# The output projection of a hybrid encoder block: every block product with both halves of the activations in one matrix multiplication, and part of VectorE's work on GpSimd

## Chip, cores, metric

One core of one Trainium2 chip. The metric is the device time of one execution in microseconds (us); the time of the kernel before is the median of 3 runs. Engines are named as in the profile: PE is TensorE, PEld its weight loads, DVE is VectorE, ACT is ScalarE, POOL is GpSimd, SP issues DMAs.

## The reference

One layer of a streaming encoder on x of 512 frames by 2048 columns, all in float32. The part that the change touches is the second of these lines, the projection by W_out with its residual, and what the next line needs of it:

```python
mixed = jnp.concatenate([o_gdn, o_rwkv], axis=-1).astype(h.dtype)
h = h + mixed @ w_out[l]
h = h + _cross_attention(_rmsnorm(h, norm_xattn[l]), _rmsnorm(mem, norm_mem[l]), ...)
```

`_rmsnorm` divides by the root of the mean of h squared over the 2048 columns, so the sum of squares of the new h has to be there when cross-attention's scores are done.

## The kernel before

All large matrix products use float32 numbers split in a high part (rounded to the type that PE multiplies fast) and a low part, the rest. A product is then high x high, high x low and low x high. ACT makes the high part (`S.copy`, line 130), DVE the low part by a subtraction (line 131).

**The output projection** is one stage. It makes h transposed, in 8 blocks `p` of 256 output columns by 512 frames. Each block is a Strassen product of 2 x 2 parts (`strassen`, from line 1334): 7 products with the constants B11, T1, T2, T3, T4, B22, B21 take the place of 8. The weight operands of the products are the four loaded parts a11, a21, a22, a12, 128 x 1024 each, and four sums of them: s1 = a21 + a22, s2 = s1 - a11, a11 - a21 (written over a21) and s4 = a12 - s2. The activation operands `comb[i][k]` (`ob` in the trace) are made ahead, 128 x 512 each: columns 0 to 255 hold the high part of 256 frames, columns 256 to 511 the low part.

**A product** (`product`) splits its weight operand into `whi` and `wlo` (three buffers each), then PE goes over 8 pieces k of 128 rows. The PSUM tile `op` is 128 x 512. There are two forms. A *narrow* product multiplies `whi` by the high half and by the low half of `ob` in two instructions of 256 columns that add into the same 256 columns of `op`. A *wide* one (its number is in `wide`) multiplies `whi` by all 512 columns in one instruction, so that the two partial results lie in the two halves of `op`, and whoever reads the product has to add both. Last, both forms multiply `wlo` by the high half, 256 columns. Before, B11, T2 and T3 of blocks 1 to 6 are wide, all others narrow.

**The results** are two tiles c1 and c2 per block (tiles `h` in the trace), made by DVE from the products, 256 columns at a time (`plus`, `add`, line 1380), one addition for each half that a product has; T1's result is added twice. ACT copies the first half of B11's result (line 1398). When the first half of a tile is complete as the last one, `gained` adds x (the residual, tile `sl`, line 1582), ACT squares the sum into a tile `sl` (line 1588) and DVE adds that to `acc` (line 1589). In the last block (`p == 7`) ACT and DVE also begin to split h for the scores (`second`, lines 133 and 134).

**What sets the order.** In this stage no order is written out by hand: a scheduler places the instructions on each engine when the kernel is built, and each engine then takes its own strictly in that order. Waits come from data and from buffers that turn: 3 for `whi` and `wlo`, 3 for a11 and a21 (`wraw`), 3 for a22 and a12 (`wraw2`), 2 for the sums s1, s2 and s4 (`ws`), 3 for `sl`, 2 PSUM banks for each tag. So s4 of a block lies where s1 lay, and s1 of the next block where s2 lay. POOL has no work in this stage.

Of the kernel before, what the change touches and what calls it, by code (L numbers as in the profile page):

```python
# [11 lines left out]
AF = mybir.ActivationFunctionType  # L12
ALU = mybir.AluOpType
# [60 lines left out]
def build(tc, I, out):  # L74
    nc = tc.nc
    V, S, GP, PE = nc.vector, nc.scalar, nc.gpsimd, nc.tensor
# [41 lines left out]
    def psb(nm, tag="mx", bufs=2):  # L118
        return tile_of(ps, [P, 512], F32, tag, nm, bufs)

    def mm(o, l, r, start=True, stop=True, again=False):
        PE.matmul(o, l, r, start=start, stop=stop, skip_group_check=again)  # L122
# [5 lines left out]
    def split(src, hi, lo, gain=None):  # L128
        if gain is None:
            S.copy(hi, src)  # L130
            V.tensor_tensor(out=lo, in0=src, in1=hi.bitcast(F32), op=ALU.subtract)  # L131
        else:
            S.activation(hi, src, AF.Copy, scale=gain)
            V.scalar_tensor_tensor(out=lo, in0=src, scalar=gain, in1=hi.bitcast(F32),
                                   op0=ALU.mult, op1=ALU.subtract)
# [227 lines left out]
    def tl(tag, w=512, bufs=1, shape=None):  # L363
        cnt[0] += 1
        return tile_of(pm, shape or [P, w], F32, tag, f"{tag}_{cnt[0]}", bufs)
# [50 lines left out]
    wq += [("w", I["wqT"][n][:, g * 1024:(g + 1) * 1024]) for n in range(KD) for g in range(2)]  # L416
    NKP, NKQ = 2 * NIN, 2 * NIN + 2 * KD
    raws, halves, used, whole, piece = {}, {}, set(), set(), {}

    def pieceload(i):  # L420
# [59 lines left out]
    acc = tl("r")  # L480
# [809 lines left out]
    hres = [hp[k // 4 * 2 + k % 2][:, k // 2 % 2] for k in range(16)]  # L1290
# [4 lines left out]
    def sl2(w=512):  # L1295
        cnt[0] += 1
        return ph.tile([P, 512], F32, tag="sl", name=f"sl{cnt[0]}", bufs=3)[:, 0:w]
# [10 lines left out]
    B11, T1, T2, T3, T4, B22, B21 = range(7)  # L1308
# [28 lines left out]
    def strassen(nm, pool, src, ks, done, used=None, first=False, wide=(), sums=None):  # L1337

        w = len(ks) * P

        def raw(p_, tag, bufs, i):
            cnt[0] += 1
            r = p_.tile([P, 1024], F32, tag=tag, name=f"{tag}_{cnt[0]}", bufs=bufs)[:, 0:w] \
                if p_ is pw else p_.tile([P, pool[1]], F32, tag=tag, name=f"{tag}_{cnt[0]}", bufs=bufs)[:, 0:w]
            if i is not None:
                nc.sync.dma_start(r, src[i])
            return r  # L1350

        def product(i, tag, a):
            cnt[0] += 1
            hi = pw.tile([P, 1024], F32R, tag="whi", name=f"whi{cnt[0]}", bufs=NWS)[:, 0:w]
            lo = pw.tile([P, 1024], F32R, tag="wlo", name=f"wlo{cnt[0]}", bufs=NWS)[:, 0:w]
            split(a, hi, lo)
            pt = psb(f"{nm}_{i}", tag)
            pa_ = pt[:, HA]
            last = len(ks) - 1
            for zs in (range(last), range(last, last + 1)) if first else (range(last + 1),):  # L1360
                for z in zs:
                    k, sl = ks[z], slice(z * P, z * P + P)
                    if i in wide:
                        mm(pt, hi[:, sl], comb[i][k], start=z == 0, stop=False)
                    else:
                        mm(pa_, hi[:, sl], comb[i][k][:, HA], start=z == 0, stop=False)
                        mm(pa_, hi[:, sl], comb[i][k][:, HB], start=False, stop=False)
                for z in zs:
                    mm(pa_, lo[:, z * P:z * P + P], comb[i][ks[z]][:, HA], start=False, stop=z == last)
            if used:  # L1370
                used(i)
            return (pa_, pt[:, HB]) if i in wide else (pa_,)

        def plus(o, a, p, op=ALU.add):
            for x in p:
                add(o, a, x, op)
                a = o

        def add(o, a, b, op=ALU.add):
            V.tensor_tensor(out=o, in0=a, in1=b, op=op)  # L1380

        def wraw2(i):
            return raw(pool[0], "wraw2", 3, i)

        def ws():
            return raw(pool[0], "ws", 2, None)

        a11 = raw(pw, "wraw", NWR, 0)
        if first:
            a12, a22 = raw(pw, "wraw", NWR, 3), raw(pw, "wraw", NWR, 2)  # L1390
            a21 = wraw2(1)
        else:
            a21 = raw(pw, "wraw", NWR, 1)
            a22, a12 = wraw2(2), wraw2(3)
        p1 = product(B11, "mx", a11)
        c1 = sums[0] if sums else sl2()
        c11, c12 = u1, u4 = c1[:, HA], c1[:, HB]
        S.copy(u1, p1[0])
        for x in p1[1:]:
            add(u1, u1, x)  # L1400
        if first:
            p2 = product(B21, "mg", a12)
            p4 = product(T4, "mx", a22)
        s1 = ws()
        add(s1, a21, a22)
        p5 = product(T1, "mg", s1)
        s2 = ws()
        add(s2, s1, a11, ALU.subtract)
        p6 = product(T2, "mm", s2)
        c2 = sums[1] if sums else sl2()  # L1410
        c21, c22 = u3, u2 = c2[:, HA], c2[:, HB]
        plus(u2, u1, p6)
        if first:
            plus(c11, u1, p2)
        plus(u4, u2, p5)
        add(a21, a11, a21, ALU.subtract)
        p7 = product(T3, "mm", a21)
        plus(u3, u2, p7)
        plus(c22, u3, p5)
        done(1, HB, c2)  # L1420
        if not first:
            p4 = product(T4, "mx", a22)
        plus(c21, u3, p4)
        done(1, HA, c2)
        s4 = ws()
        add(s4, a12, s2, ALU.subtract)
        p3 = product(B22, "mg", s4)
        plus(c12, u4, p3)
        done(0, HB, c1)
        if not first:  # L1430
            p2 = product(B21, "mm", a12)
            plus(c11, u1, p2)
        done(0, HA, c1)
# [13 lines left out]
    def spread(*which):  # L1447
        for i, k in which:
            comb[i][k] = (btile if k < 3 or i == B21 and k < 6 else act_tile)(f"ob{i}_{k}")
            place(i, k, *pair[k])  # L1450
# [100 lines left out]
            S.activation(sq, hres[n], AF.Square)  # L1551
            V.tensor_tensor(out=acc, in0=acc, in1=sq, op=ALU.add)

    hh_, hl_, sqsum = [], [], []

    def second(n):
        hi, lo = act_tile(f"hh{n}"), act_tile(f"hl{n}")
        split(hres[n], hi, lo, col("norm_xattn", n))
        hh_.append(hi)
        hl_.append(lo)  # L1560

    for p in range(8):
        xs = [None, None]

        def used(i):
            if i == T1:
                if p == 0:
                    spread((B22, 6), (B22, 7))
                for j in (1, 0):
                    xs[j] = sl2()  # L1570
                    nc.sync.dma_start(xs[j], I["xT"][:, 2 * p + j, :])
            elif i == T2 and p == 0:
                spread((B21, 6), (B21, 7))
                sqsum.append(ph.tile([P, T], F32, tag="acc", name="acc1", bufs=1))
            if p == 7 and i in (T2, T3):
                for n in range(2) if i == T2 else range(2, 4):
                    second(n)

        def gained(j, half, c):
            if half is HB:  # L1580
                return
            V.tensor_tensor(out=c, in0=c, in1=xs[j], op=ALU.add)
            acc = sqsum[0]
            if p == 0 and j:
                S.activation(acc, c, AF.Square)
            else:
                sq = sl2()
                S.activation(sq, c, AF.Square)
                V.tensor_tensor(out=acc, in0=acc, in1=sq, op=ALU.add)

        strassen(f"op{p}", (pz, 1024), [I["w_out"][p, i] for i in range(4)], list(range(8)), gained, used,
                 wide=(B11, T2, T3) if 0 < p < 7 else (), sums=hres[2 * p:2 * p + 2])
    pz_cm.__exit__(None, None, None)
    pl_cm = tc.tile_pool(name="pl", bufs=1, reuse_waits="tile")
    pl = pl_cm.__enter__()
# [103 lines left out]
    acc = ph.tile([P, T], F32, tag="acc", name="acc2", bufs=1)  # L1699
# [75 lines left out]
    xs = lambda u: range(2 * u[3], 2 * u[3] + 2) if len(u) > 3 else range(4)  # L1775
    units = [("u", p, 0) for p in range(32)] + [("d", e, m, *y) for e in range(4) for m in range(2) for y in (((0,), (1,)) if (e, m) in INSITU else ((),))]
    raws, sums, halves = {}, {}, {}
# [641 lines left out]
```

## Time and profile before

| what | us |
|---|---|
| median of 3 runs (2904.82, 2906.90, 2906.92) | 2906.9 |
| the profiled execution | 2904.46 |
| its span, first to last instruction | 2902.7 |
| the output projection in it, from 1305 to 1465 | 160 |

The profile is of one execution. Its page gives the busy time of each engine, and the trace behind it answers views: busy time by windows of time, groups of instructions by line, who waited for whom, the chain of work that ended last, and a timeline of single instructions. In a timeline row stand the start in us from the span's start, the duration in us (of all instructions of the row), the engine, the line, the operation, the tiles as output<-inputs with buffer numbers left out, and in brackets the idle time ahead of it with what ended it. On an engine the next instruction may start while the one before still ends, so that the price of one in a row of many is the distance from start to start.

### The profile page before, as it was taken

The page shows a single profiled execution, that of the slowest core. Times are in us where ns is not written, and L with a number is a line of the kernel's source. Part 1 is how long each engine was busy: PE and PEld are TensorE (multiplying, and loading weights), DVE is VectorE, ACT ScalarE, POOL GpSimd, SP SyncE. Part 2 cuts the span into 40 slices and gives each one's busy share as a digit, 9 for nine tenths or more (in the row PEclk, how much of TensorE's full clock was granted, in tenths as well). Part 3 has the DMA queues.
Part 4 walks back from the last instruction along what each step waited for, and adds up shares of the span by engine and source line. Part 5 has one row for each costly group of instructions (what it writes and reads, how often), then busy time and mean ns, then how long its engine had stood idle before and what let it go on. Part 6 is the DMA issues. An engine that isn't in the chain of part 4 may idle for free.

```text
span 2902.7 us, 49242 instructions
## 1 busy us (share of the span) xinstructions
PE 2870.4 (99%) x18794; PEld 2420.3 (83%) x18794; DVE 2330.4 (80%) x3547; ACT 1570.0 (54%) x2233; POOL 223.6 (8%) x547
## 2 busy tenths in 40 slices
PE   8999999999999999999999999999999999999998
PEld 7877877787877888889988888888888888888887
DVE  7787787787887877769956898898998878787888
ACT  6454555555655655564445656555555645454544
POOL 0213213213223000000000000000000000000000
PEclk9999999999999999999999999999999999999999
DMA  5646656656666788784423354565566868978733
GB/s 190 175 139 184 164 156 181 160 150 187 176 163 188 219 249 280 227 286 159 127 92 95 106 163 152 193 199 193 186 201 191 283 225 278 295 257 272 270 100 109
DMA packets 319773, 553.02 MB, mean 191 GB/s; under 512 B 100968, under 2 KB 186220, under 8 KB 319536
## 3 DMA queue, kind: packets, MB, share of 16 engines
q1 hardware_dynamic: 292144, 518.41, 58.0%
q10 hardware_dynamic: 27392, 31.46, 3.1%
q8 instruction: 147, 2.41, 0.3%
q14 instruction: 90, 0.74, 0.1%
HBM read 443.45 MB, written 106.31 MB: 189 GB/s over the span
## 4 chain that ended last, share of the span: by engine, by line
PE 93%; DMA 3%; DVE 2%; ACT 1%; issue 1%; POOL 0%; ACTq 0%; SPq 0%; DVEq 0%; POOLq 0%
PE py L256 22%; PE mxu L256 12%; PE mgu L256 6%; PE mgd L256 6%; PE mxd L256 6%; PE op L122 6%; PE vp L122 3%; PE sc L122 3%; PE at L122 3%; PE mmd L256 3%; PE kp L256 3%; PE mmu L256 3%; PE scrd L256 3%; PE scgd L256 3%; PE kq L256 3%; PE vo L122 1%
## 5 line engine op out<-in xcount | busy, mean ns | idle before, releaser
L256 ACT CAST whi<-wraw 128x1024 fp32r<-128x1024 f32 (+1 forms) x366 | 383.7, 1049 | 399.8 <-PE py L256 146.8
L256 DVE TENSOR_TENSOR wlo<-wraw,whi 128x1024 fp32r<-128x1024 f32 (+1 forms) x366 | 450.4, 1231 | 102.7 <-ACT whi L256 92.9
L256 PE MATMUL py<-xhi,whi 128*128 128x512 f32 x928 | 372.2, 401 | 7.8 <-ACT xhi L256 7.8
L256 PE MATMUL py<-xlo,whi 128*128 128x512 f32 x928 | 373.7, 403 | 0.0
L256 PE MATMUL py<-xhi,wlo 128*128 128x512 f32 x928 | 372.9, 402 | 0.0
L256 ACT CAST whi<-w 128x1024 fp32r<-128x1024 f32 x176 | 185.4, 1054 | 203.9 <-PE mxu L256 48.3
L256 DVE TENSOR_TENSOR wlo<-w,whi 128x1024 fp32r<-128x1024 f32 x176 | 214.8, 1221 | 51.5 <-ACT whi L256 49.5
L256 PE MATMUL mxu<-cb,whi 128*128 128x512 f32 x1016 | 255.0, 392 | 0.0
L256 PEld LDWEIGHTS py<-xhi,whi 128*128 128x128 f32 x928 | 175.0, 189 | 42.1 <-ACT xhi L256 7.8
L256 PEld LDWEIGHTS mxu<-cb,whi 128*128 128x128 f32 x1016 | 182.8, 189 | 32.7
L256 PEld LDWEIGHTS py<-xlo,whi 128*128 128x128 f32 x928 | 175.0, 189 | 35.5 <-DVE xlo L256 0.9
L256 PEld LDWEIGHTS py<-xhi,wlo 128*128 128x128 f32 x928 | 175.1, 189 | 35.1 <-issue 1.8
L131 DVE TENSOR_TENSOR wlo<-wraw,whi 128x1024 fp32r<-128x1024 f32 x112 | 136.6, 1221 | 45.5 <-ACT whi L130 42.5
L130 ACT CAST whi<-wraw 128x1024 fp32r<-128x1024 f32 x112 | 117.7, 1051 | 85.5 <-PE op L122 29.1
L256 PEld LDWEIGHTS mxu<-cb,wlo 128*128 128x128 f32 x1016 | 138.7, 190 | 10.5 <-DVE wlo L256 0.7
L256 PE MATMUL mxu<-cb,wlo 128*128 128x256 f32 x1016 | 142.2, 282 | 0.3 <-DVE wlo L256 0.3
L256 ACT ACT_TABLE_LOAD x87 | 111.6, 1283 | 36.4 <-DVE suml_gn L256 15.5
L256 PE MATMUL mgu<-cb,whi 128*128 128x512 f32 x512 | 129.4, 394 | 1.4 <-ACT whi L256 1.3
L256 PE MATMUL mxd<-whi,cb 128*128 128x512 f32 x512 | 126.7, 389 | 0.0
L256 PE MATMUL mgd<-whi,cb 128*128 128x512 f32 x512 | 126.5, 389 | 0.0
L256 ACT CAST whi<-ws 128x1024 fp32r<-128x1024 f32 x75 | 78.9, 1052 | 75.4 <-PE mgu L256 49.2
L122 PE MATMUL op<-ob,whi 128*128 128x256 f32 (+1 forms) x752 | 115.3, 304 | 0.0
(946 smaller groups left out, 6452.3 us busy)
## 6 DMA issues: line engine op xcount, KB each, us to landing
wraw<-in_w_in SPq DMA_DIRECT2D x116, 512.0 KB, 4.5
wraw<-in_w_up SPq DMA_DIRECT2D x65, 512.0 KB, 3.8
w<-in_w_up SPq DMA_DIRECT2D x63, 512.0 KB, 3.9
ds<-in_w_dm SPq DMA_DIRECT2D x128, 205.0 KB, 4.0
sd_s<-ds SPq DMA_DIRECT2D x128, 205.0 KB, 5.2
wraw<-sd_s SPq DMA_DIRECT2D x51, 512.0 KB, 5.1
w<-sd_s SPq DMA_DIRECT2D x50, 512.0 KB, 5.0
w<-in_w_dm SPq DMA_DIRECT2D x48, 512.0 KB, 5.1
```

The lines of the kernel that those rows point to most:

```text
L122: PE.matmul(o, l, r, start=start, stop=stop, skip_group_check=again)
L130: S.copy(hi, src)
L131: V.tensor_tensor(out=lo, in0=src, in1=hi.bitcast(F32), op=ALU.subtract)
L256: f(*a, **k)
```

## The change

Every product of every block is wide, those of blocks 0 and 7 too. POOL computes two of the four weight sums, a11 - a21 and s4, which are also written earlier in the code: a11 - a21 right behind s1, s4 right behind the product T2. For blocks 0 to 6 POOL also adds the residual and adds the squares to `acc`; block 7 keeps both on DVE. The squares are no longer issued with the residual: they are put in a list, and issued behind the next product B22 or T2. The first square of all goes to `acc` directly.

```diff
@@ strassen
         s1 = ws()
         add(s1, a21, a22)
+        GP.tensor_tensor(out=a21, in0=a11, in1=a21, op=ALU.subtract)
         p5 = product(T1, "mg", s1)
         s2 = ws()
         add(s2, s1, a11, ALU.subtract)
         p6 = product(T2, "mm", s2)
+        s4 = ws()
+        GP.tensor_tensor(out=s4, in0=a12, in1=s2, op=ALU.subtract)
...
-        add(a21, a11, a21, ALU.subtract)
         p7 = product(T3, "mm", a21)
...
-        s4 = ws()
-        add(s4, a12, s2, ALU.subtract)
         p3 = product(B22, "mg", s4)
@@ used
         def used(i):
+            if i in (B22, T2):
+                for f in later:
+                    f()
+                later.clear()
@@ gained
-            V.tensor_tensor(out=c, in0=c, in1=xs[j], op=ALU.add)
-            acc = sqsum[0]
-            if p == 0 and j:
-                S.activation(acc, c, AF.Square)
+            G = GP if p < 7 else V
+            G.tensor_tensor(out=c, in0=c, in1=xs[j], op=ALU.add)
+
+            def squared():
+                if not sqsum[1:]:
+                    sqsum.append(1)
+                    S.activation(sqsum[0], c, AF.Square)
+                else:
+                    sq = sl2()
+                    S.activation(sq, c, AF.Square)
+                    G.tensor_tensor(out=sqsum[0], in0=sqsum[0], in1=sq, op=ALU.add)
+
+            if p < 7:
+                later.append(squared)
             else:
-                sq = sl2()
-                S.activation(sq, c, AF.Square)
-                V.tensor_tensor(out=acc, in0=acc, in1=sq, op=ALU.add)
+                squared()

         strassen(...,
-                 wide=(B11, T2, T3) if 0 < p < 7 else (), sums=hres[2 * p:2 * p + 2])
+                 wide=range(7), sums=hres[2 * p:2 * p + 2])
```

How this moves instructions shows best on DVE where block 5 ends (its products T4, T1, B22 and B21 are `op_4`, `op_1`, `op_5` and `op_6`), block 6 is under way (`wlo` of `ws` are its splits for T1 and T2) and block 7 begins (its s1 is the sum of two `wraw`). Before, in DVE's order:

```order
L1582 TENSOR_TENSOR h_12819<-h_12819,sl_15756 128x512
L1380 TENSOR_TENSOR h_12818<-h_12818,op_5_15851 128x256
L131 TENSOR_TENSOR wlo_15945<-ws_15942,whi_15944 128x1024
L1589 TENSOR_TENSOR acc_14693<-acc_14693,sl_15842 128x512
L1380 TENSOR_TENSOR ws_16062<-wraw_757_15917,ws_15977 128x1024
L1380 TENSOR_TENSOR h_12818<-h_12818,op_6_15881 128x256
L131 TENSOR_TENSOR wlo_15980<-ws_15977,whi_15979 128x1024
L1582 TENSOR_TENSOR h_12818<-h_12818,sl_15758 128x512
L1380 TENSOR_TENSOR ws_16166<-wraw_16130,wraw_774_16132 128x1024
```

The same place after the change:

```order
L1380 TENSOR_TENSOR h_12818<-h_12818,op_5_15679 128x256
L131 TENSOR_TENSOR wlo_15760<-ws_15756,whi_15759 128x1024
L1380 TENSOR_TENSOR h_12818<-h_12818,op_5_15679 128x256
L1380 TENSOR_TENSOR h_12818<-h_12818,op_6_15705 128x256
L131 TENSOR_TENSOR wlo_15787<-ws_15784,whi_15786 128x1024
L1380 TENSOR_TENSOR h_12818<-h_12818,op_6_15705 128x256
L1380 TENSOR_TENSOR ws_15946<-wraw_15917,wraw_773_15919 128x1024
L131 TENSOR_TENSOR wlo_15817<-wraw_15727,whi_15816 128x1024
L1380 TENSOR_TENSOR h_12820<-h_12820,op_0_15737 128x256
L131 TENSOR_TENSOR wlo_15842<-wraw_755_15729,whi_15841 128x1024
```

The two residual additions (1582), the squares' addition (1589) and s4 (the sum of `wraw_757` and `ws`) are gone from DVE, and `op_5` and `op_6` are added in two halves, with a split between the halves. The splits for T3 and T4 (the last two `wlo`) follow s1 with one addition from PSUM between them.

On POOL the difference begins behind its last instruction of an earlier stage; the names are those of blocks 0, 1 and 2:

```order
 L256 COPY sgi_10571<-sgi_10571 32x256
-L2414 UNCONDITIONAL_BRANCH
-L2414 ISA
+L1406 TENSOR_TENSOR wraw_14579<-wraw_14577,wraw_14579 128x1024
+L1412 TENSOR_TENSOR ws_14672<-wraw_650_14583,ws_14642 128x1024
+L1406 TENSOR_TENSOR wraw_14777<-wraw_14775,wraw_14777 128x1024
+L1587 TENSOR_TENSOR h_12815<-h_12815,sl_14638 128x512
+L1412 TENSOR_TENSOR ws_14860<-wraw_666_14781,ws_14834 128x1024
+L1587 TENSOR_TENSOR h_12814<-h_12814,sl_14640 128x512
+L1406 TENSOR_TENSOR wraw_14967<-wraw_14965,wraw_14967 128x1024
+L1596 TENSOR_TENSOR acc_14671<-acc_14671,sl_14857 128x512
```

Where the program ended for POOL, 43 instructions stand now: 16 weight sums (1406 and 1412), 14 residual additions (1587) and 13 additions of squares (1596). In the steady order of a block, POOL takes the first residual of a block (with its squares behind it), then s4 of the next block, then the second residual, then a11 - a21 of the block after that, then the second squares. On ACT the order of instructions is the same as before; on SP the loads of weights and of x are the same in number, and the loads of x now wait for POOL instead of DVE to give back a tile `sl`.

More of the change, by code (lines that the diff above doesn't have):

```diff
@@ L1552, in finish @@
             V.tensor_tensor(out=acc, in0=acc, in1=sq, op=ALU.add)
-    hh_, hl_, sqsum = [], [], []
+    hh_, hl_, sqsum, later = [], [], [], []
     def second(n):
```

## The prediction

> **What bounds the kernel now.** I read the page's first lines, then the stage that the change touches, then what is waited for in it.
>
> ```profile
> span 2902.7 us, 49242 instructions
> PE 2870.4 (99%) x18794; PEld 2420.3 (83%) x18794; DVE 2330.4 (80%) x3547; ACT 1570.0 (54%) x2233; POOL 223.6 (8%) x547
> ```
>
> TensorE (PE) has work for 99% of the span, so a faster neighbour gains little; what makes PE wait is lost in full. The view by windows puts the stage (the output projection) and the 40 us behind it side by side; its columns are the window, its length, then busy us and instructions of PE, weight loads, VectorE (DVE), ScalarE (ACT), GpSimd (POOL), the granted clock and DMA.
>
> ```profile
> 1305.00:1465.00 160.00, 160.00 (x1202) 153.74 (x1201) 153.27 (x204) 77.29 (x94) 0.00 (x0) 1.00 0.44 138
> 1465.00:1505.00 40.00, 40.00 (x183) 33.24 (x183) 16.17 (x20) 13.89 (x18) 0.00 (x0) 1.00 0.33 106
> ```
>
> PE has no gap in these 160 us, and the chain of waits is one piece of PE there. But DVE is next: 153 of 160 us. The waits of the stage say who leads:
>
> ```profile
> ACT whi L130 <- PE op L122: 57.2, 35, 2.0
> DVE h L1380 <- PE op L122: 3.9, 11, 0.5
> PEld op L122 <- ACT whi L130: 0.2, 1, 0.2
> ```
>
> ACT waits 57 us for PE to give a weight buffer back, PE waits 0.2 us for anybody: the splits run ahead as far as three buffer pairs let them. The stage is PE's, with DVE 4% short of being the bound. So the change is worth what it takes from PE, until DVE needs longer per block than PE.
>
> **PE's part.** Four products of one block, on PE's timeline (start, duration, instructions):
>
> ```profile
> 1365.29 2.00 PE L122 MATMUL op<-ob,whi 128*128 128x512 f32 x8
> 1367.13 1.12 PE L122 MATMUL op<-ob,wlo 128*128 128x256 f32 x8
> 1368.08 2.08 PE L122 MATMUL op<-ob,whi 128*128 128x256 f32 x16
> 1370.00 1.12 PE L122 MATMUL op<-ob,wlo 128*128 128x256 f32 x8
> 1370.96 2.00 PE L122 MATMUL op<-ob,whi 128*128 128x512 f32 x8
> 1385.19 2.00 PE L122 MATMUL op<-ob,whi 128*128 128x512 f32 x8
> ```
>
> From start to start a wide product takes 1368.08 - 1365.29 = 2.79 us, a narrow one 1370.96 - 1368.08 = 2.88, and the next block begins at 1385.19: 19.90 us a block. Narrow before are all seven products of blocks 0 and 7 and four in each of the six others, 38 in all. Making them wide saves 38 x 0.085 = **3.2 us** of PE time at most, 0.1% of the run, and a block is then 7 x 2.79 = 19.55 us, if nobody else needs longer.
>
> **DVE's part.** Its timeline in the same stage:
>
> ```profile
> 1385.72 0.41 DVE L1380 TENSOR_TENSOR h<-h,op 128x256 f32<-128x256 f32 x1
> 1386.05 1.22 DVE L131 TENSOR_TENSOR wlo<-ws,whi 128x1024 fp32r<-128x1024 f32 x1
> 1387.19 0.69 DVE L1582 TENSOR_TENSOR h<-h,sl 128x512 f32<-128x512 f32 x1
> 1387.79 1.22 DVE L1380 TENSOR_TENSOR ws<-wraw,wraw 128x1024 f32<-128x1024 f32 x1
> 1388.93 0.68 DVE L1589 TENSOR_TENSOR acc<-acc,sl 128x512 f32<-128x512 f32 x1
> ```
>
> From start to start: an add from PSUM 0.33, a split or a weight sum 1.14, a residual or squares' add 0.60. Before, a block has 7 splits and 4 sums, 10 adds, and 2 + 2 of 0.60: 12.5 + 3.3 + 2.4 = 18.2 us. After, 7 splits and 2 sums (10.3), and 15 adds (5.0), since each wide product's second half is added too (the products T1 twice): **15.2 us**. By this DVE has 4.3 us of air under PE's 19.55.
>
> **GpSimd's part.** Per block it gets two sums of 1024 columns and four instructions of 512. The nearest rows, from an earlier stage:
>
> ```profile
> 569.74 1.31 POOL L256 TENSOR_TENSOR gEs<-gE,cst 128x512 f32<-128x512 f32 x1
> 570.97 0.48 POOL L256 MEMSET sgi<- 32x256 f32 x2
> 342.32 0.29 POOL L256 TENSOR_TENSOR sr<-sr,sr 64x55 f32<-64x55 f32 x1
> ```
>
> 512 columns take 1.24 us to the next start. From 55 to 512 columns it is (1.31 - 0.29) / 457 = 2.2 ns a column, so 1024 take 1.24 + 1.14 = 2.38 us. No row shows this size: twice the 512 row gives 2.48 as the upper end, and 2.0 ns a column (the slope of the smaller sizes) 2.26 as the lower; I take 2.38. Sum: 4 x 1.24 + 2 x 2.38 = **9.7 us** a block. Alone that fits twice into 19.55. The Trainium skill (GPSIMD Engine Reference, section 3.1, Elementwise) has 4497 ns for 2048 columns of this kind; half of it, 2.25 us, is an estimate by that page, with which the block below would be 0.26 us and the run 2 us shorter; the trace has no row of that size to test it.
>
> **The two together.** They don't run beside each other freely. The rows of POOL and DVE at three places:
>
> ```profile
> 569.76 2.37 DVE L256 TENSOR_TENSOR wlo<-wraw,whi 128x1024 fp32r<-128x1024 f32 x1 [1.73 <-ACT whi L256]
> 341.24 0.28 POOL L256 TENSOR_TENSOR sr<-sr 64x60 f32<-64x60 f32 x1
> 113.84 1.37 POOL L256 TENSOR_TENSOR sr<-sr 64x60 f32<-64x60 f32 x1
> 113.84 1.23 DVE L256 TENSOR_TENSOR wlo<-wraw,whi 128x1024 fp32r<-128x1024 f32 x1 [5.23 <-PE py L256]
> 798.08 1.30 POOL L256 TENSOR_TENSOR gEs<-gE,cst 128x512 f32<-128x512 f32 x1
> 798.00 0.69 DVE L256 TENSOR_TENSOR y<-py,rstd 128x512 f32<-128x512 f32 x1 [1.52 <-PE py L256]
> 798.86 1.60 DVE L256 TENSOR_TENSOR wlo<-wraw,whi 128x1024 fp32r<-128x1024 f32 x1 [0.17 <-ACT whi L256]
> ```
>
> The split that starts 0.02 us after a POOL instruction (569.74, above) takes 2.37 us where it takes 1.22 alone: it stands still until POOL is done. At 113.84 the split is first, and POOL needs 1.37 us where it needs 0.28. At 798 the DVE instruction with one input in PSUM (py) runs through beside POOL, neither the longer for it; the split behind it is held up again. So a DVE instruction with both inputs in SBUF and a POOL instruction exclude each other for their whole length, whoever is first; an add from PSUM doesn't mind.
>
> Splits and sums are such instructions, and DVE takes them in its written order. I go through one block in that order, with each POOL instruction starting when its input is there. Behind the first residual add DVE has one add from PSUM half under way, then a split: it stands 1.05 us. Behind the squares' add, two adds, then a split: 0.57. During s4 (2.38) one add, then the next block's s1, which needs the buffer that s4 still reads: 2.05. The second residual add starts as s4 ends, ahead of s1: 1.24. During a11 - a21 (2.38) one add, then a split: 2.05. During the second squares' add one add, then a split: 0.91. Together **7.9 us**: of 9.7 us of POOL only some 1.85 us lie beside adds. DVE's block is then 15.2 + 7.9 = 23.1 us, PE's is 19.55, and three buffer pairs can't carry 3.5 us a block for long. The 3.2 us won on PE vanish under it.
>
> The same for all eight blocks (block 0 has no earlier residual but four more splits of activations, block 7 keeps its residual on DVE): 8 x (23.1 - 19.9) = **25.6 us** more. The stage behind has DVE busy 16 of 40 us, so PE neither gives time back there nor loses more. The order of ACT's instructions doesn't change; the squares wait for POOL now, and behind the first the split of T2 is queued, but DVE can't take that earlier than 0.57 us after its adds, so I cost it at nothing (1.24 us a block if the residual comes later). The loads of x wait for POOL too, ahead of weights on SP's queue, for tiles used a block later: nothing.
>
> **Rivals.** *No exclusion at this place* (not slower): 1024 columns beside 1024 columns are not among the rows; if splits stay at 1.22 us, PE binds with 19.55 us: 2904.5 - 3.2 = 2901 us. It decides where DVE's split stays under 1.4 us beside a POOL sum. Against it speak all three places; 6%. That the work isn't moved at all is excluded: the order of POOL's instructions has 43 new ones.
>
> *Exclusion, but hidden*: POOL falls beside adds only. Then 10.3 + 9.7 = 20.0 us a block, 0.1 more than now: 2905 us. DVE's adds stand in groups of one to four, POOL's starts follow DVE's own results; 6%.
>
> *The clock falls as well.* PE idles 3.5 us a block, some 2 us in one piece ahead of T4, whose split waits behind a11 - a21. One place in the trace has such waits:
>
> ```profile
> 900.00:920.00 20.00, 16.58 (x108) 13.41 (x106) 11.37 (x23) 13.01 (x24) 7.79 (x21) 1.00 0.74 189
> 920.00:940.00 20.00, 16.74 (x272) 13.68 (x273) 14.09 (x24) 9.48 (x16) 7.69 (x19) 0.91 0.60 178
> PE kp L256 <- ACT whi L256: 2.4, 1, 2.4
> PE ri7u L256 <- DVE k L256: 2.0, 1, 2.0
> ```
>
> After two waits of over 2 us the clock stays at 1.00, after one of 2.0 us the next window has 0.91: 1.8 us lost. At every block, on the path: 8 x 1.8 = 14 us, 2945 us. But DVE is the bound then, so PE can lose 1.8 us unseen; 13%. The Trainium skill (TensorE: Matmul & The Clock Gate, Part 1) wants an idle window of some 3.4 us for the fall to half speed; by that rule no gap of mine is long enough and the cost is nothing, by the row at 920 a shorter one did it once.
>
> **How the numbers follow.** The profiled execution took 2904.5 us, its span and 1.8 us around it; 2904.5 + 25.6 = 2930.1. The median of the runs shown is 2.4 us above that execution, so I say **2931 us**, with 75% for this mechanism. Its ends: if none of POOL's time lies beside adds, 24.9 us a block, 8 x 5.0 = 40, 2945, and the upper POOL price adds 2; if 3.5 us lie beside them and the lower price holds, 15.2 + 9.4 - 3.5 = 21.1, 8 x 1.2, some 2915. The range 2916 to 2947 holds that and half of the clock's case; out are the two cases at 2901 and 2905. A measurement here tells 0.2% (5.8 us) from no change. Slower by more: 90% (the forecast, the clock's case, most of the tails); within 0.2%: 9% (2901, 2905, a low tail at 2910); faster: 1%, since PE's whole saving is 3.2 us.
>
> **What would show it.** In the profile after: op products start 23 us apart by block; splits of the stage have a mean near 1.9 us instead of 1.22 while adds stay at 0.41; PE waits for wlo, which it never does now; POOL's 1024 rows at 2.4 us when first. Wrong would be the exclusion if splits stay at 1.22; the cover if the block is 20 to 21 us; the clock if PEclk is below 1 in the stage.

## The result, and the profile after

The changed kernel takes 2925.9 us (median of 6 runs, 2924.8 to 2928.0), the kernel before 2904.2 us on the same chip (6 runs, 2902.2 to 2906.9). The ratio is 1.0075, its 95% interval 1.0062 to 1.0087: slower by 18 to 25 us, where 2931 us were forecast.

The page's first lines of the changed kernel (of an execution of 2924.8 us):

```profile
span 2923.0 us, 48740 instructions
PE 2874.3 (98%) x18490; PEld 2403.8 (82%) x18490; DVE 2353.0 (80%) x3550; ACT 1568.9 (54%) x2233; POOL 321.1 (11%) x590
```

The span is 20.3 us longer, PE's busy time hardly changed: PE waits now. Where, the windows over the output projection say (columns as in the prediction; a window in the middle and the last one):

```profile
1385.00:1405.00 20.00, 18.12 (x103) 15.42 (x104) 18.01 (x24) 7.72 (x10) 10.42 (x6) 1.00 0.34 106
1465.00:1485.00 20.00, 17.51 (x91) 14.84 (x89) 17.69 (x27) 10.19 (x15) 6.69 (x3) 0.91 0.20 61
```

Neither engine is busy throughout: PE waits for DVE's splits, and DVE in turn for POOL, while the profile counts a part of that as idle and a part as busy. The view of waits over 1305 to 1490, in which PE before waited for nobody longer than 0.2 us in all:

```profile
PEld op L122 <- DVE wlo L131: 24.1, 23, 2.0
PE op L122 <- DVE wlo L131: 14.6, 21, 1.6
DVE ws L1380 <- POOL ws L1412: 9.8, 5, 2.0
```

One block of PE, from its first product (1369.69) to the next block's (1392.20); the rows left out follow each other without a gap:

```profile
1369.69 2.00 PE L122 MATMUL op<-ob,whi 128*128 128x512 f32 x8
...
1378.07 2.00 PE L122 MATMUL op<-ob,whi 128*128 128x512 f32 x8
1381.64 1.21 PE L122 MATMUL op<-ob,wlo 128*128 128x256 f32 x8 [1.57 <-DVE wlo L131]
1382.69 2.00 PE L122 MATMUL op<-ob,whi 128*128 128x512 f32 x8
1384.99 1.21 PE L122 MATMUL op<-ob,wlo 128*128 128x256 f32 x8 [0.29 <-DVE wlo L131]
1386.04 2.00 PE L122 MATMUL op<-ob,whi 128*128 128x512 f32 x8
...
1391.14 1.22 PE L122 MATMUL op<-ob,wlo 128*128 128x256 f32 x8 [0.31 <-DVE wlo L131]
1392.20 2.00 PE L122 MATMUL op<-ob,whi 128*128 128x512 f32 x8
```

The block takes 22.51 us where PE's seven wide products need 19.55. The gaps stand ahead of the `wlo` of T3 (the fourth product), T4 and B21: the high part had been there, DVE's low part came late. Eight blocks begin at 1302.42, 1325.42, 1347.16, 1369.69, 1392.20, 1414.72, 1437.23 and 1459.75, and the first score product follows at 1483.61: 23.0, 21.7, five of 22.5, and 23.9 us. The stage is 181.2 us long, 21.2 more than the 159.95 of before.

DVE over the same block:

```profile
1371.42 2.20 DVE L131 TENSOR_TENSOR wlo<-ws,whi 128x1024 fp32r<-128x1024 f32 x1
1374.21 1.66 DVE L131 TENSOR_TENSOR wlo<-ws,whi 128x1024 fp32r<-128x1024 f32 x1
1375.79 0.41 DVE L1380 TENSOR_TENSOR h<-h,op 128x256 f32<-128x256 f32 x1
1378.16 2.29 DVE L1380 TENSOR_TENSOR ws<-wraw,wraw 128x1024 f32<-128x1024 f32 x1 [1.96 <-POOL ws L1412]
1380.38 1.21 DVE L131 TENSOR_TENSOR wlo<-wraw,whi 128x1024 fp32r<-128x1024 f32 x1
1381.84 3.09 DVE L131 TENSOR_TENSOR wlo<-wraw,whi 128x1024 fp32r<-128x1024 f32 x1
1385.19 1.98 DVE L131 TENSOR_TENSOR wlo<-ws,whi 128x1024 fp32r<-128x1024 f32 x1
```

And POOL:

```profile
1371.25 1.29 POOL L1587 TENSOR_TENSOR h<-h,sl 128x512 f32<-128x512 f32 x1 [7.67 <-DVE h L1380]
1373.28 1.50 POOL L1596 TENSOR_TENSOR acc<-acc,sl 128x512 f32<-128x512 f32 x1 [0.74 <-ACT sl L1595]
1374.74 3.38 POOL L1412 TENSOR_TENSOR ws<-wraw,ws 128x1024 f32<-128x1024 f32 x1
1378.08 1.29 POOL L1587 TENSOR_TENSOR h<-h,sl 128x512 f32<-128x512 f32 x1
1380.53 3.32 POOL L1406 TENSOR_TENSOR wraw<-wraw,wraw 128x1024 f32<-128x1024 f32 x1 [1.16 <-DVE ws L1380]
1383.80 2.28 POOL L1596 TENSOR_TENSOR acc<-acc,sl 128x512 f32<-128x512 f32 x1
```

Read them against each other. The split at 1371.42 starts 0.17 us after the residual and takes 2.20 us, not 1.22. The sum s4 (1374.74) starts half a microsecond behind a split and takes 3.38 us; it had to wait for that split to end. The s1 at 1378.16, which may only begin when s4 has given its buffer back, starts 0.08 us after the second residual and takes 2.29. Of POOL and a DVE instruction with two inputs in SBUF one always stands while the other works, and it does not matter which came first; only the add from PSUM (1375.79) keeps its 0.41 us while s4 runs. The groups of the whole stage (1305 to 1486) say the same:

```profile
L131 DVE TENSOR_TENSOR wlo<-wraw,whi 128x1024 fp32r<-128x1024 f32 x31 | 53.4, 1727 | 0.5 <-ACT whi L130 0.5
L131 DVE TENSOR_TENSOR wlo<-ws,whi 128x1024 fp32r<-128x1024 f32 x24 | 47.4, 1977 | 0.0
L1380 DVE TENSOR_TENSOR h<-h,op 128x256 f32<-128x256 f32 x118 | 44.7, 411 | 2.4 <-ACT h L1398 2.1
```

Before (1305 to 1465) the same groups were:

```profile
L131 DVE TENSOR_TENSOR wlo<-wraw,whi 128x1024 fp32r<-128x1024 f32 x32 | 38.9, 1219 | 4.1 <-ACT whi L130 4.1
L131 DVE TENSOR_TENSOR wlo<-ws,whi 128x1024 fp32r<-128x1024 f32 x24 | 29.2, 1218 | 0.0
L1380 DVE TENSOR_TENSOR h<-h,op 128x256 f32<-128x256 f32 x73 | 29.8, 414 | 4.1 <-PE op L122 3.9
```

The splits have grown by half (mean of one from 1219 and 1218 ns to 1727 and 1977), the adds not at all.

### The profile page after: what moved, and what is told of

It is laid out like the page before. It is cut to its first block, busy times and chain, and to the rows that moved or that the text cites. A ratio compares the mean times of both kernels' runs of the same rounds, so it can differ in the third digit from the quotient of the medians.

```text
span 2923.0 us, 48740 instructions
## 1 busy us (share of the span) xinstructions
PE 2874.3 (98%) x18490; PEld 2403.8 (82%) x18490; DVE 2353.0 (80%) x3550; ACT 1568.9 (54%) x2233; POOL 321.1 (11%) x590
## 3 DMA queue, kind: packets, MB, share of 16 engines
q8 instruction: 145, 2.38, 0.3%
## 5 line engine op out<-in xcount | busy, mean ns | idle before, releaser
L131 DVE TENSOR_TENSOR wlo<-wraw,whi 128x1024 fp32r<-128x1024 f32 x112 | 152.5, 1363 | 40.8 <-ACT whi L130 37.6
L122 PE MATMUL op<-ob,whi 128*128 128x512 f32 x448 | 113.4, 395 | 2.5 <-ACT whi L130 2.5
```

## The experiments

Theories: **exclusion** (the prediction's); **late data** (POOL's results simply come too late for who needs them, whether or not DVE is held up); **wide adds** (five more adds a block on DVE are the cost); **order** (the later squares and earlier sums stand badly in the queues). Each run is set against runs of the kernel before on its own chip, so the second number of a pair differs a little from run to run.

**1. Exclusion without any new data.** The kernel before, with POOL reading each finished half block for nobody:

```diff
             V.tensor_tensor(out=c, in0=c, in1=xs[j], op=ALU.add)
+            for i in range(4):
+                GP.tensor_tensor(out=dum, in0=c, in1=c, op=ALU.add)
```

> The kernel before, with eight additions of 512 columns per block put on GpSimd that read the finished tile h and write a scratch tile that nobody reads; the result is that of the kernel before. Exclusion: 8 x 1.24 = 9.9 us of GpSimd per block hold up VectorE's splits and sums; with some 2 us beside additions from PSUM a block takes 18.2 + 7.9 = 26 us instead of 19.9, so 35 to 60 us more, 2940 to 2965 us. Late data (TensorE waits because GpSimd's results come late) and wide products (VectorE's extra additions): nothing waits for this work and no product is changed, so 2904 us within 0.2%.

Measured: 2940.0 us against 2902.2, ratio 1.0127 (1.0113 to 1.0141), +38 us, the low edge of what was expected: from the second block on a block takes 23.1 to 25.6 us where 26 were expected. DVE and POOL in it:

```profile
1397.73 6.45 POOL L1585 TENSOR_TENSOR dum<-h 128x512 f32<-128x512 f32 x4 [8.94 <-DVE h L1583]
1397.83 2.02 DVE L131 TENSOR_TENSOR wlo<-ws,whi 128x1024 fp32r<-128x1024 f32 x1
1399.77 1.52 DVE L1592 TENSOR_TENSOR acc<-acc,sl 128x512 f32<-128x512 f32 x1
1401.22 2.06 DVE L1380 TENSOR_TENSOR ws<-wraw,ws 128x1024 f32<-128x1024 f32 x1
1403.20 0.41 DVE L1380 TENSOR_TENSOR h<-h,op 128x256 f32<-128x256 f32 x1
```

Nobody waits for `dum`, and nothing is wide that wasn't; yet each split, sum and squares' add beside POOL grows by 0.8 us, and POOL's four take 6.45 us where four alone take some 5. Late data can't make that. The clock is 0.95 in this stage (1305 to 1485), so a part of the 38 us may be PE's.

**2. The same with instructions that read next to nothing.** Nine memsets in the place of the four reads:

```diff
+            GP.tensor_tensor(out=dum[:, 0:8], in0=c[:, 0:8], in1=c[:, 0:8], op=ALU.add)
+            for i in range(9):
+                GP.memset(dum[:, 8:512], float(i))
```

> The same as the idle reads, but per half block one addition of 8 columns and nine memsets of 504 columns, which read nothing and keep GpSimd busy for about as long (9 x 0.5 us). Exclusion by what both read: memsets beside a split cost nothing (a memset of 0.48 us stands beside an undisturbed split of 1.22 us in the trace of before), 2904 to 2908 us. Exclusion of any GpSimd instruction: as the idle reads, 2940 us or more.

Measured: 2900.9 against 2902.2 us, ratio 0.9995 (0.9986 to 1.0004). This run says nothing on memsets: they touch other columns than the small addition, so nothing tied them to it, and the scheduler put all 144 ahead of the stage. It was made again with the memset over the whole tile (`GP.memset(dum, float(i))`), which ties each group to its half block:

> The kernel before, with one GpSimd addition of 8 columns and behind it nine memsets of 512 columns (about 0.52 us each) on the same tile behind each half block's residual, so that they can't be placed anywhere else: some 9 to 10 us of GpSimd a block that read almost nothing, where idle_read had 10.3 us that read. If only GpSimd instructions that read exclude DVE: the stage stays at 19.9 us a block, DVE's splits at 1.22 us beside the memsets, ratio 0.999 to 1.001 of before. If any GpSimd instruction excludes DVE: as idle_read, some 35 to 40 us more, ratio 1.012 to 1.014, splits of 1.3 to 1.7 us (a memset is short, so each hold-up is under 0.5 us, but there are nine in a row).

Measured: 2901.6 against 2901.6 us, ratio 0.9999 (0.9990 to 1.0008). The memsets now lie in the stage (129 of 528 ns from 1305 to 1465):

```profile
1368.98 1.22 DVE L1380 TENSOR_TENSOR ws<-wraw,wraw 128x1024 f32<-128x1024 f32 x1
1369.21 1.05 POOL L1584 TENSOR_TENSOR dum<-h 128x8 f32<-128x8 f32 x1 [0.23 <-DVE h L1583]
1370.32 5.21 POOL L1586 MEMSET dum<- 128x512 f32 x9
1371.06 1.21 DVE L131 TENSOR_TENSOR wlo<-wraw,whi 128x1024 fp32r<-128x1024 f32 x1
1372.43 1.23 DVE L131 TENSOR_TENSOR wlo<-wraw,whi 128x1024 fp32r<-128x1024 f32 x1 [0.16 <-ACT whi L130]
1373.58 1.22 DVE L1380 TENSOR_TENSOR wraw<-wraw,wraw 128x1024 f32<-128x1024 f32 x1
```

Two splits and a sum run their 1.2 us beside nine memsets, while the tiny addition, which reads, took 1.05 us behind a sum of DVE (0.20 us when nothing is in its way). So it isn't POOL's activity: what holds DVE up are POOL's instructions that read. The Trainium skill (SBUF — State Buffer, Who interferes with whom) says just that: DVE instructions with two inputs in SBUF contend with GpSimd instructions that read SBUF, not with those that only write it, and the order of issue decides which of the two is blocked; all of these rows agree.

**3. The changed kernel with POOL's dependences but hardly any reads.** Each of POOL's instructions becomes an addition of 8 columns and memsets of about the same length:

```diff
+    def fill(out, x, y):
+        w = out.shape[1]
+        GP.tensor_tensor(out=out[:, 0:8], in0=x[:, 0:8], in1=y[:, 0:8], op=ALU.add)
+        for i in range(2):
+            GP.memset(out[:, 8:w], float(i))
+        GP.memset(out[:, 8:w // 2], 0.5)
...
-        GP.tensor_tensor(out=a21, in0=a11, in1=a21, op=ALU.subtract)
+        fill(a21, a11, a21)
```

(and so s4, the residual and the squares of blocks 0 to 6).

> The changed kernel, with every GpSimd instruction of the stage replaced by an addition of its first 8 columns and memsets over the rest that take about as long (the weight sums, the residual and the squares' sum are left out, so h is not the reference's). Every wait for data and buffers stays. Exclusion: VectorE's 15.2 us and the 2 us that s1 waits for s4's buffer fit into TensorE's 19.55 us; 2899 to 2906 us. Late data: as the changed kernel, 2926 us.

Measured: 2900.6 against 2902.2 us, ratio 0.9995 (0.9985 to 1.0005). Its windows show PE without a gap from the fourth block on:

```profile
1365.00:1385.00 20.00, 20.00 (x116) 17.57 (x115) 18.24 (x30) 8.46 (x10) 9.28 (x19) 1.00 0.50 156
1385.00:1465.00 80.00, 80.00 (x462) 70.45 (x461) 67.64 (x106) 40.30 (x49) 34.73 (x67) 1.00 0.38 119
```

Late data falls: who waits for POOL here waits for instructions of about the same length in the same places (those of s4 take 3.9 us from 1386.54 to 1390.42, where s4 takes 3.38 in the changed kernel), and the 21.7 us are gone. The four blocks from 1366.76 to 1444.97 take 19.55 us each, the figure forecast for seven wide products; three waits in the first three blocks (0.84, 0.92 and 1.27 us) hide that saving in the whole.

**4. Wide products alone, all work on DVE** (the kernel before with `wide=range(7)`):

> The kernel before with all products wide and nothing on GpSimd. VectorE then needs 18.2 + 5 x 0.33 = 19.9 us a block beside TensorE's 19.55, with little air: 19.6 to 20.8 us a block, 2902 to 2911 us by exclusion. If the extra additions of wide products were the cause: most of the 22 us, 2920 us or more.

Measured: 2908.3 against 2902.2 us, ratio 1.0019 (1.0011 to 1.0028). Its first three blocks take 19.8 us, the next four 20.8 to 20.9, the last 23.6: with five more adds DVE has 15.2 + 4.7 = 19.9 us of work a block (4.7 us is what POOL's work takes on DVE: 2 x 1.14 + 4 x 0.60), and with its wait for ACT (0.95 us a block in the late ones) that is more than PE's 19.55.

**5. The changed kernel with the wide products of before** (`wide=(B11, T2, T3) if 0 < p < 7 else ()`):

> The changed kernel with the products wide only as before (B11, T2, T3 of blocks 1 to 6); GpSimd's work stays. Exclusion: VectorE has 5 x 0.33 = 1.65 us less to add, and some of these additions stood beside GpSimd, so a block takes 21.5 to 22.3 us instead of 22.5: 2915 to 2925 us. Wide products as the cause: 2904 us.

Measured: 2922.3 against 2900.7 us, ratio 1.0075 (1.0060 to 1.0090). Most of the price is there without the added halves, so "wide adds" is not the cause. That the whole of it is there is in part chance: the middle blocks take 21.85 us, as expected, and not 22.5, and the first one makes up for it (26.9 us, with the clock at 0.91 from 1305 to 1325).

**6 and 7. Half of POOL's work.** Only the two sums on POOL (`G = V`), and only the residual and squares (`V.tensor_tensor` for both sums):

> The changed kernel with the residual and the squares' sum back on VectorE; only the two weight sums stay on GpSimd. Exclusion: VectorE has 15.2 + 2.4 = 17.6 us, and is held up by the two sums for 3.8 us as in the changed kernel: 21.4 us a block, 12 us more than before, 2912 to 2921 us. Late data: TensorE waits for the sums, so all of it, 2926 us.

> The changed kernel with the two weight sums back on VectorE; the residual and the squares' sum stay on GpSimd. Exclusion: 15.2 + 2.3 = 17.5 us of VectorE and 3.3 us of waits behind the four instructions of 512 columns: 20.8 to 21.6 us a block, 2910 to 2918 us. Late data: TensorE never waits for residual or squares, 2901 to 2906 us.

Measured: sums 2918.4 us, ratio 1.0064 (1.0048 to 1.0081); residual and squares 2914.9 us, ratio 1.0049 (1.0034 to 1.0064), both against 2900.7. The middle blocks take 21.5 and 21.2 us, within what exclusion gave. Each half alone costs; no single wait carries the loss. In the run with the sums, a sum of POOL starts first and the next split pays for it:

```profile
1393.72 2.73 POOL L1412 TENSOR_TENSOR ws<-wraw,ws 128x1024 f32<-128x1024 f32 x1 [13.34 <-DMA wraw<-in_w_out]
1394.43 3.10 DVE L131 TENSOR_TENSOR wlo<-ws,whi 128x1024 fp32r<-128x1024 f32 x1
```

**8. A third buffer for the sums** (`raw(pool[0], "ws", 3, None)`), so that s1 needn't wait for s4's end:

> The changed kernel with three buffers instead of two for the weight sums, so that s1 of the next block needs not wait for s4 to have read s2 (a wait of 1.96 us a block in the profile of the changed kernel). Exclusion: s1 reads two tiles in SBUF and stands behind s4 all the same, so nothing is won, 2920 to 2928 us. Late data or buffers as the cause: up to 8 x 1.96 = 16 us less, 2910 us.

Measured: 2927.8 against 2900.7 us, ratio 1.0094 (1.0079 to 1.0109): no time gained, which is what was expected, but by luck: it came about in another way, and the run does not isolate the buffer. With three buffers the scheduler chose another order for POOL: s4 stands ahead of the first residual, not behind its squares. s1 no longer stands beside s4, and its 9.8 us of waits for POOL are gone with most of its hold-up (a mean of 1990 ns in the changed kernel):

```profile
L1380 DVE TENSOR_TENSOR ws<-wraw,wraw 128x1024 f32<-128x1024 f32 x7 | 9.3, 1329 | 5.2 <-DMA wraw<-in_w_out 4.6 <-DVE h L1380 0.5
1451.57 2.08 PE L122 MATMUL op<-ob,wlo 128*128 128x256 f32 x8 [3.29 <-DVE wlo L131]
```

In their place s1 and s4 wait for weights to be loaded (4.6 and 28.8 us in all), other DVE instructions are held up (the split that ends PE's wait of 3.29 us takes 3.25), and the clock is lower: 0.91 in three of the 20 us windows from 1305 on and 0.83 in one, where the changed kernel has 0.91 in one. Its blocks take between 19.6 and 25.9 us. That waits for POOL's buffers are not the cause rests on run 3, which keeps them all.

**9. The changed code with everything back on DVE** (both sums and `G = V`), for the order:

> The changed kernel in its new order of code (a11 - a21 and s4 earlier, squares later), with all of GpSimd's work put back on VectorE. Exclusion: nothing left to exclude; VectorE's 19.9 us a block bind a little as with wide products alone, 2904 to 2912 us. If the new order were a cause of its own: 2915 us or more.

Measured: 2910.8 against 2900.8 us, ratio 1.0038 (1.0023 to 1.0054). It loses what wide products on DVE lose (the intervals of runs 4 and 9 overlap), not 21.7 us. No run takes the later squares and the earlier sums apart.

**10. What is left of the gain.** Six products wide in blocks 0 to 6, T1 narrow, all on DVE (`wide=(B11, T2, T3, T4, B22, B21) if p < 7 else ()`):

> The kernel before with six of the seven products wide (all but T1, whose second half costs two additions) in blocks 0 to 6, block 7 narrow as before, all on VectorE. TensorE wins 3 x 0.085 us in blocks 1 to 6 and 6 x 0.085 in block 0, 2.0 us in all; VectorE needs 18.2 + 3 x 0.33 = 19.2 us a block beside TensorE's 19.65. 2 us less than before, at the edge of what can be measured. If VectorE's additions cost more than their time: no gain or 1 to 4 us more.

Measured: 2902.1 against 2900.8 us, ratio 1.0005 (0.9997 to 1.0014). Five of its blocks take 19.64 us as expected, but PE waits for ACT's high part once in the first block (0.96 us) and once in the last (1.01), and no gain is left that can be measured. No run beat the kernel before.

## Why the prediction was right, point by point

**What bounds the stage.** Right: PE led, DVE was 4% behind. Run 4 shows how little that was: five adds more, and the late blocks are DVE's.

**PE's part.** Right: 19.55 us a block in run 3. It doesn't show in the changed kernel, whose blocks are DVE's.

**DVE's and POOL's own times.** Right: 1024 columns on POOL, when nothing is in its way, are 2.42 us here (2.38 estimated from the 512-column row; the estimate by half of the figure in the Trainium skill's GPSIMD Engine Reference, section 3.1, was 2.25):

```profile
1329.35 2.42 POOL L1412 TENSOR_TENSOR ws<-wraw,ws 128x1024 f32<-128x1024 f32 x1 [1.22 <-issue]
```

In the middle blocks POOL stands too: its six instructions take 13.1 us there, not 9.7.

**The exclusion.** Right, as the cause: runs 1, 2 (the second version) and 3 tell it from late data and from POOL's mere activity, 5 and 9 from the wide adds and from the order.

**Its size.** Each of the six stalls is where it was put, from the rows of DVE above:

| stall | predicted, us | measured, us |
|---|---|---|
| split behind the first residual | 1.05 | 2.20 - 1.22 = 0.98 |
| split behind the first squares' add | 0.57 | 1.66 - 1.22 = 0.44 |
| s1 behind s4 | 2.05 | 1.96 |
| s1 behind the second residual | 1.24 | 2.29 - 1.21 = 1.08 |
| split behind a11 - a21 | 2.05 | 3.09 - 1.22 = 1.87 |
| split behind the second squares' add | 0.91 | 1.98 - 1.22 = 0.76 |

Together 7.1 us, not 7.9. In the five that lengthen an instruction, the hold-up is 0.13 to 0.14 us shorter than the rest of POOL's instruction: at the first one 1371.25 + 1.29 - 1371.42 = 1.12 us of the residual were left and the split took 0.98 more. That is 0.7 of the missing 0.8 us. The rows in the prediction have it already: at 569.76 there were 1.29 us left and 1.15 more, at 798.86 0.52 left and 0.38 more. "For their whole length" was read 0.14 us too long from them. My reading, not tested, is that an instruction that is held up has part of its start behind it when the other engine ends. With it DVE's block is 15.2 + 7.1 = 22.3 us, and 22.5 were measured in the middle. The term of the sum that was mis-sized is this one: 8 x (22.5 - 19.9) = 21 us in the place of 25.6, and the ratio gives 21.7. A slip in the last step took a little off the forecast: 2930.1 and the 2.4 us of the median make 2932.5, not 2931.

**PE's wait in one piece.** The prediction put some 2 us ahead of T4, whose split stands behind a11 - a21. That failed in place and size: PE waits 1.57 us ahead of T3, since T3's split is queued behind the late s1, 0.29 ahead of T4 and 0.31 ahead of B21.

**The stage behind, costed at nothing.** Wrong by 1.8 us: ahead of early scores PE waits 0.40 and 1.43 us for additions to h (`PE sc L122 <- DVE h L1380`), which it did not before. With the 21.2 us of the stage that makes 23.1; the profiled execution had reached the stage 2.7 us sooner (1302.42 against 1305.10), so 20.4 are left, and its span is 20.3 us longer.

**The squares on ACT, costed at nothing.** Right in the middle blocks, wrong once. In block 7, POOL's second residual of block 6 was itself held up by a split (2.28 us), ACT's square waited for it, and T4's high part was queued behind the square, the copy of B11 and two splits of h:

```profile
1468.15 2.28 POOL L1587 TENSOR_TENSOR h<-h,sl 128x512 f32<-128x512 f32 x1
1470.46 0.63 ACT L1595 ACTIVATE sl<-h 128x512 f32<-128x512 f32 x1 [5.30 <-POOL h L1587]
...
1472.48 1.03 ACT L130 CAST whi<-wraw 128x1024 fp32r<-128x1024 f32 x1
```

PE waited 2.49 us there, and the clock fell behind it (last section), which cost 1.66 us. From 1469.97 to 1473.57 PE lost 0.16 us more than the wait (3.60 us, where 0.95 are usual), and 19.55 + 2.49 + 1.66 + 0.16 are that block's 23.86 us. Block 7 thus costs about what was forecast (23.1) by luck, for another reason than forecast; in run 4, with nothing on POOL, it takes 23.6 us too.

**The rivals.** *No exclusion* gives 2901 us, and run 3, in which little is read, shows that figure; in the changed kernel the splits' means of 1.73 and 1.98 us rule it out. *Hidden exclusion* needed blocks of 20.0 us. *The clock* fell in one block of eight, not in each; in the others PE has no wait of the 2 us that this rival needs (the longest is 1.61).

## What to carry to other kernels

Before work is moved from DVE to POOL, look whether DVE's instructions beside it read two operands from SBUF: then the two engines take turns, and POOL's time is to be added to DVE's but for what lies beside instructions that read PSUM. Here 4.7 us of work a block left DVE and 7.1 us of standing still came for it. A queue that has such a held-up instruction ahead of others passes its delay on: the cost shows two engines away, as PE waiting for a split that was never touched.

## What was not expected of the hardware

The granted clock fell once in the changed kernel, in block 7, behind a wait that the prediction did not have:

```profile
1473.57 3.25 PE L122 MATMUL op<-ob,whi 128*128 128x512 f32 x8 [2.49 <-ACT whi L130]
1478.02 2.01 PE L122 MATMUL op<-ob,whi 128*128 128x512 f32 x8
```

This product takes 4.45 us from start to start where 2.79 are usual, so 1.66 us are lost beside the wait itself, and the window has 0.91. The Trainium skill (TensorE: Matmul & The Clock Gate, Part 1) wants an idle window of some 3.4 us for the fall; this one came after 2.49 us, and before the change one of 2.0 us was followed by 0.91, two of over 2 us by 1.00. In run 8 the clock fell behind a wait of 1.80 us too (0.91 from 1405 to 1425), and in run 1 one of 2.10 us left it at 1.00 in the same window. So it is not the length of the wait alone; what decides it is open, since no run here varied a wait by itself.
